# Attention's stages farther apart, one ring for the weights, norms cut into steps: a change to the order of work in a decoder layer on one core

## The chip, the cores and the metric

The kernel runs on one core of a Trainium2 chip. The metric is device time in microseconds (us) of one execution; a kernel's time is the median of several. The core has a matrix engine (TensorE, PE in the rows; PEld is its weight load), three engines for the rest (VectorE or DVE, ScalarE or ACT, GpSimd or POOL), and SyncE (SP), whose only work here is to issue DMAs. Every engine, SP's queue among them, executes its own list of instructions strictly in order, so one that waits holds up all behind it.

## The reference

One layer of a decoder on 2048 tokens of width 1024, all in float32:

```python
mod = silu(c) @ w_ada + b_ada                   # six vectors: shift, scale, gate, twice
shift1, scale1, gate1, shift2, scale2, gate2 = jnp.split(mod, 6, axis=-1)
h = modulate(rms_norm(x, g_mix), shift1, scale1)
proj = h @ w_in                                 # u, v of the gMLP | q (8 heads) | k, v (2 heads)
out_a = chunked_sgu(gelu(z_a), w_spatial, b_spatial)            # chunks of 128 tokens, causal
out_b = sliding_window_sink_attention(q, k, v, sinks, positions) # window 128, rotary
x = x + gate1 * (concat([out_a, out_b]) @ w_out)
h2 = modulate(rms_norm(x, g_ffn), shift2, scale2)
x = x + gate2 * (square(relu(h2 @ w_ff1)) @ w_ff2)              # width 4096
return rms_norm(x, g_final)
```

## The kernel before

The tokens lie in four slabs of 512 (slab 0 to 3), features on the 128 partitions. Every large product is made of three matmuls (`mm3`): an operand is split into a high part (ACT copies it to the matmul's type) and a low part (DVE subtracts), and high times high, high times low and low times high are added up in PSUM. Each slab passes through `in_qkv` (q, k, v, with rotary in `rotate`), `in_vu` (the gMLP), `attention`, `mix_build` and `out_proj` (which also adds up the squares for the next norm). The two feed-forward halves, `ffn_c` (w_ff1) and `ffn_d` (w_ff2), work on a pair of slabs p at once by a scheme of seven products in place of eight; `h2_build` makes their inputs. `ffn_d` goes through products i = 1, 6, 5, 3, 7, 4, 2, each in eight chunks of 24 matmuls; after 7 and after 2 a slab of the output is complete and `final_norm` runs.

The parts are generators that yield between pieces of work, and the program weaves them: `weave(main, side, per=3)` takes three steps of `side` after each step of `main`, `zipped` takes turns, `ratio(a, 3, b, 1)` three of one and one of the other. A scheduler then makes each engine's list from that order. Within `attention` there are eight units (128 tokens and one k/v head each), and each passes four stages: q (split q: tile `qst`), p (scores `sc` on PE, softmax to `pr` on DVE and ACT), t (transposes `tpp` on PE, split to `pc` on ACT and DVE, causal masks to `pp` and `pc` on POOL) and o (`ov` on PE, `os` on ACT and DVE, then a DMA to `mixb`). One loop turns them:

```python
for t in range(n + 3):
    for i in (3, 2, 1, 0):
        if 0 <= t - i < n:
            stages[i](t - i)
            yield
```

so a unit's stage follows three yields after the one before. Tiles come from rings of fixed size, and an allocation waits for the oldest use to end: `wr` (4 tiles of 4 KB a partition) takes raw weights, `wk` (8) their split parts, `xl` (4 of 2 KB) x tiles and the modulation weights `adar`, `m2` (60 of 2 KB) nearly everything else. `ada_rest(ci)` makes one of the modulation vectors 2 to 5: 16 loads, 16 scalings on ACT, 14 additions on POOL (`acc`), 8 small matmuls (`modp`). A norm is `finish` (four small matmuls `msp`, then POOL's power) and `spread` (a diagonal `dg` on DVE, a matmul `bcp`, a copy to `rbc` on ACT). Slab 2's q, k, v are made early, parked in DRAM (`away`) and loaded again (`back`, `qkv_back`); the slabs in the tuple `LATER` do this.

From 907 us on, `ffn_d(0)` is the main line and everything that remains of slabs 2 and 3 (`beside`) is woven into it at three steps a chunk, then `h2_build(1)` at one step a chunk.

Of the kernel before, what the change touches and what calls it, by code (L numbers as in the profile page):

```python
# [49 lines left out]
def hybrid_block(ctx, tc, x_l, c_l, pos, wada0, wada, vec, win, wsT, bs, sinks, wout, w1, w2, rope_c, y_l):  # L50
# [14 lines left out]
    def wk(name, shape=None):  # L65
        return sb.tile(shape or [P, D], F32R, name=name, tag="wk", bufs=NWK)

    def wr(name, shape=None):
        return sb.tile(shape or [P, D], F32, name=name, tag="wr", bufs=NWR)

    def wk4(name, shape):
        return sb.tile(shape, F32R, name=name, tag="wr", bufs=NWR)
# [111 lines left out]
    class Stat:  # L184
# [23 lines left out]
        def spread(self, out=None, tag="ov"):  # L208
            nb = self.n // P
            parts = [small("rh", [P, NB], F32R), small("rl", [P, NB], F32R)]  # L210
            dve.tensor_copy(out=parts[0][:, :nb], in_=self.rs[:, :nb])
# [2 lines left out]
            for i, r in enumerate(parts):
                dg = t2("dg", F32R, [P, NB, P])
                dve.tensor_tensor(out=dg[:, :nb], in0=ident.unsqueeze(1).broadcast_to([P, nb, P]),
                                  in1=r[:, :nb].unsqueeze(2).broadcast_to([P, nb, P]), op=ALU.mult)
                pe.matmul(out=bp[:, :nb], lhsT=ones_r, rhs=dg[:, :nb], start=i == 0, stop=i == 1)
# [1 line left out]
            act.activation(out=rbc[:, :self.n], in_=bp[:, :nb], func=AF.Copy)  # L220
            return rbc[:, :self.n]

        def bcast(self, out=None, tag="ov"):
            self.finish(tag)
            return self.spread(out, tag)
# [566 lines left out]
    def ffn_c(p, forms):  # L792
        raws, wfs = {}, {}

        def split(src, name, home=wk):
            hi, lo = home(name), home(name)
            act.activation(out=hi, in_=src, func=AF.Copy)
            dve.tensor_tensor(out=lo, in0=src, in1=hi, op=ALU.subtract)  # L798
            return hi, lo
# [89 lines left out]
    def ffn_d(p):  # L889
# [26 lines left out]
        for i in (1, 6, 5, 3, 7, 4, 2):  # L916
# [5 lines left out]
            for c in range(8):  # L922
                wraw, araw = wr("w2w"), wr("aw", [P, 2, T])
# [7 lines left out]
                wh, wl, ah, al = wk("w2h"), wk("w2l"), wk("ah", [P, 2, T]), wk("al", [P, 2, T])  # L931
                act.activation(out=wh, in_=wraw, func=AF.Copy)  # L932
                dve.tensor_tensor(out=wl, in0=wraw, in1=wh, op=ALU.subtract)  # L933
                act.activation(out=ah, in_=araw, func=AF.Copy)  # L934
                dve.tensor_tensor(out=al, in0=araw, in1=ah, op=ALU.subtract)  # L935
# [297 lines left out]
```

## Time and profile before

| | |
|---|---|
| median of 3 executions | 2215.06 us (2214.13 to 2216.72) |
| the profiled execution, its own time | 2211.44 us |
| its span, first to last instruction | 2209.7 us (1.7 us lie around it) |
| PE busy | 1965.2 us, 89% of the span |
| DVE, ACT, POOL busy | 1398.8, 936.4 and 244.7 us |
| mean granted TensorE clock | 0.945 |
| DMA | 475.24 MB, mean 215 GB/s |

PE is the engine to follow: it is busy 89% of the time, and the rest of the time it waits for one of the others. Two numbers say what a wait costs: the idle time itself, and the granted clock (PEclk), which is 1.00 (2.4 GHz) in steady work and shows 0.50 (1.2 GHz) in pieces around the waits.

### The profile page before, as it was taken

How to read it: one execution, taken by the hardware profiler on the slowest of the kernel's cores; microseconds unless marked ns; L12 is line 12 of the kernel's file. 1: busy time of each engine (PE TensorE's matmuls, PEld its weight loads, DVE VectorE, ACT ScalarE, POOL GpSimd, SP SyncE). 2: the span in 40 equal slices, each digit the busy share in tenths (PEclk: the TensorE clock that was granted, in tenths of full speed). 3: DMA queues.
4: the chain of work that ended last, by engine and by line, in shares of the span. 5: the costliest groups of instructions: out<-in, count | busy, mean ns of one | idle time of the engine just before them, and what ended most of it. 6: DMA issues, size and time to landing. Idle time of an engine off the chain costs nothing.

```text
span 2209.7 us, 26145 instructions
## 1 busy us (share of the span) xinstructions
PE 1965.2 (89%) x8852; PEld 1604.4 (73%) x8852; DVE 1398.8 (63%) x2342; ACT 936.4 (42%) x1618; POOL 244.7 (11%) x290
## 2 busy tenths in 40 slices
PE   5988788779799999968998998898799999999997
PEld 4777665558677788757786876677688888888775
DVE  7766566624877866666556565279776666444665
ACT  3534444343554444542344243237344444433432
POOL 5223101251030000011001022000000000000000
PEclk9999889789899999989999998999899999999998
DMA  9874474488379945879875764668344445666653
GB/s 365 317 284 149 147 260 152 136 288 289 99 251 308 310 156 167 265 241 317 293 250 177 243 196 160 212 211 282 126 162 157 158 148 175 207 197 216 212 190 133
DMA packets 230391, 475.24 MB, mean 215 GB/s; under 512 B 23617, under 2 KB 81089, under 8 KB 230257
## 3 DMA queue, kind: packets, MB, share of 16 engines
q1 hardware_dynamic: 229136, 472.85, 63.1%
q8 instruction: 70, 1.15, 0.2%
q0 software_dynamic: 1120, 0.72, 0.1%
q14 instruction: 65, 0.52, 0.1%
HBM read 343.78 MB, written 129.70 MB: 214 GB/s over the span
## 4 chain that ended last, share of the span: by engine, by line
PE 49%; DMA 10%; DVE 9%; issue 2%; ACT 2%; POOL 1%; SPq 0%; DVEq 0%; POOLq 0%; ACTq 0%
PE mm L296 16%; PE mm L295 15%; PE mm L297 15%; DMA a<-in_w_dram 3%; DMA w2d<-a 2%; DMA s<-w2d 1%; DVE al L935 1%; DVE hw L726 1%; DMA r<-in_w_dram 1%; DVE w2l L933 1%; DVE y L983 1%; PE ov L646 0%; DVE x L900 0%; DVE ssum L194 0%; ACT pr L606 0%
## 5 line engine op out<-in xcount | busy, mean ns | idle before, releaser
L296 PE MATMUL mm<-al,w2h 128*128 128x512 f32 x896 | 358.9, 401 | 15.7 <-DVE al L935 15.7
L297 PE MATMUL mm<-ah,w2l 128*128 128x512 f32 x896 | 356.4, 398 | 0.0
L295 PE MATMUL mm<-ah,w2h 128*128 128x512 f32 x896 | 313.1, 401 | 12.8 <-DVE pr L591 6.7
L932 ACT ACTIVATE w2h<-w2w 128x1024 fp32r<-128x1024 f32 x112 | 118.6, 1058 | 311.1 <-PE mm L296 270.3
L933 DVE TENSOR_TENSOR w2l<-w2w,w2h 128x1024 fp32r<-128x1024 f32 x112 | 137.8, 1230 | 168.0 <-ACT w2h L932 167.2
L296 PEld LDWEIGHTS mm<-al,w2h 128*128 128x128 f32 x896 | 173.3, 193 | 56.8 <-DVE al L935 21.1
L295 PEld LDWEIGHTS mm<-ah,w2h 128*128 128x128 f32 x896 | 172.0, 193 | 50.9 <-ACT ah L934 7.0
L297 PEld LDWEIGHTS mm<-ah,w2l 128*128 128x128 f32 x896 | 173.0, 193 | 36.2
L295 PE MATMUL mm<-h,whi 128*128 128x512 f32 x320 | 130.8, 425 | 22.5 <-ACT h L233 8.0
L205 POOL TENSOR_TENSOR rs<-ms,mhalf 128x4 f32<-128x4 f32 x12 | 15.8, 1318 | 1195.5 <-DVE ms L203 1195.5
L934 ACT ACTIVATE ah<-aw 128x1024 fp32r<-128x1024 f32 x112 | 117.4, 1048 | 65.5 <-PE mm L296 56.2
L935 DVE TENSOR_TENSOR al<-aw,ah 128x1024 fp32r<-128x1024 f32 x112 | 137.1, 1224 | 7.7 <-ACT ah L934 7.2
L297 PE MATMUL mm<-h,wlo 128*128 128x512 f32 x320 | 131.5, 412 | 5.5 <-POOL wlo L263 3.4
L296 PE MATMUL mm<-h,whi 128*128 128x512 f32 x320 | 132.2, 414 | 0.6 <-DVE h L234 0.6
L295 PE MATMUL mm<-mix,whi 128*128 128x512 f32 x256 | 108.6, 425 | 18.9 <-DVE x L684 13.1
L295 PE MATMUL mm<-hw,wa 128*128 128x512 f32 x256 | 103.2, 403 | 20.5 <-ACT hw L725 12.0
L296 PE MATMUL mm<-mix,whi 128*128 128x512 f32 x256 | 106.1, 415 | 1.8 <-DVE mix L673 1.7
L629 POOL TENSOR_SCALAR_AFFINE_SELECT pp<-pc 128x512 fp32r<-128x512 f32 x60 | 49.1, 818 | 522.0 <-ACT pc L623 509.7
L297 PE MATMUL mm<-mix,wlo 128*128 128x512 f32 x256 | 105.2, 411 | 0.0
L296 PE MATMUL mm<-hw,wa 128*128 128x512 f32 x256 | 102.1, 399 | 1.1 <-DVE hw L726 1.1
L295 PE MATMUL mm<-hw,wb 128*128 128x512 f32 x256 | 100.1, 391 | 2.4 <-DVE w L857 2.3
L297 PE MATMUL mm<-hw,wa 128*128 128x512 f32 x256 | 101.4, 398 | 0.3 <-DVE wa L798 0.3
(255 smaller groups left out, 4451.8 us busy)
## 6 DMA issues: line engine op xcount, KB each, us to landing
aw<-ad SPq DMA_DIRECT2D x112, 512.0 KB, 4.6
r<-in_w_dram SPq DMA_DIRECT2D x64, 512.0 KB, 4.2
w2w<-w2d SPq DMA_DIRECT2D x64, 512.0 KB, 3.6
ad<-wt SPq DMA_DIRECT2D x96, 256.0 KB, 4.3
a<-in_w_dram SPq DMA_DIRECT2D x96, 256.0 KB, 4.7
w2w<-in_w_dram SPq DMA_DIRECT2D x96, 256.0 KB, 3.8
xt<-in_x_dram SPq DMA_DIRECT2D x80, 256.0 KB, 4.2
adar<-in_wada_dram SPq DMA_DIRECT2D x64, 256.0 KB, 4.0
```

Of the source, the lines that this page charges most:

```text
L205: self.pow = pool.tensor_tensor(out=rs[:, :nb], in0=ms[:, :nb], in1=mhalf[:, :nb], op=ALU.pow)
L295: pe.matmul(out=out, lhsT=wh, rhs=h[0], start=first, stop=False, **kw)
L296: pe.matmul(out=out, lhsT=wh, rhs=h[1], start=False, stop=False, **kw)
L297: last_mm[0] = pe.matmul(out=out, lhsT=wl, rhs=h[0], start=False, stop=last, **kw)
L629: pool.affine_select(out=o, in_=i, pattern=[[0, 4], [-1, P]], compare_op=ALU.is_gt, fill=0.0, base=0, channel_multiplier=1)
L726: dve.tensor_tensor(out=lo, in0=f, in1=hi, op=ALU.subtract)
L932: act.activation(out=wh, in_=wraw, func=AF.Copy)
L933: dve.tensor_tensor(out=wl, in0=wraw, in1=wh, op=ALU.subtract)
L934: act.activation(out=ah, in_=araw, func=AF.Copy)
L935: dve.tensor_tensor(out=al, in0=araw, in1=ah, op=ALU.subtract)
L983: dve.scalar_tensor_tensor(out=y, in0=x, scalar=gfin[:, d:d + 1], in1=rbc, op0=ALU.mult, op1=ALU.mult)
```

## The change

It touches five things. (1) The stages of a step of attention run in the order q, p, t, o in place of o, t, p, q, so that a unit's stage follows five yields after the one before. (2) `wr` is gone; raw weights, split weights, the modulation weights (now two tiles a load, 512 KB) and two x tiles of the last norm share one ring `wk` of 12. (3) Norms are cut into `finish`, `diag` and `cast` with yields between; `final_norm` is a generator, stepped between the chunks of `ffn_d` or woven into `ffn_c(1)`. (4) Modulation vector 3 is made beside attention of slab 0, and vector 4 beside `in_qkv(2)`; `out_proj(1)` runs with nothing beside it. (5) Slab 3 joins `LATER`.

```diff
-NT, NM, NWK, NWR, NXL = 9, 60, 8, 4, 4
+NT, NM, NWK, NXL = 9, 60, 12, 4
-LATER = (2,)
+LATER = (2, 3)
...
-                raw = sb.tile([P, T], F32, name="adar", tag="xl", bufs=NXL)
-                nc.sync.dma_start(out=raw, in_=wada[ci - 2, half, k])
+                if k % 2 == 0:
+                    two = wk("adar", F32, [P, 2, T])
+                    nc.sync.dma_start(out=two, in_=wada[ci - 2, half, k:k + 2].rearrange("k p t -> p k t"))
+                raw = two[:, k % 2]
...
-        def spread(self, out=None, tag="ov"):
+        def diag(self):
...
+        def cast(self, out=None, tag="ov"):
...
+        def spread(self):
+            self.diag()
+            return self.cast()
...
-        raw = wr("raw")
+        raw = wk("raw", F32)
...
-            for i in (3, 2, 1, 0):
+            for i in range(4):
                 if 0 <= t - i < n:
                     stages[i](t - i)
                     yield
...
         for s in (2 * p, 2 * p + 1):
-            rb2[s] = rb2[s].spread()
+            rb2[s].diag()
+        yield
+        for s in (2 * p, 2 * p + 1):
+            rb2[s] = rb2[s].cast()
         yield
...
-                raws[j] = wr("r1"), wr("r2")
+                raws[j] = wk("r1", F32), wk("r2", F32)
...
-                xs[r, t, b] = m2("x3", F32)
+                if src is x2d:
+                    xs[r, t, b] = m2("x3", F32)
+                else:
+                    two = wk("x3w", F32, [P, 2, T]) if b % 2 == 0 else two
+                    xs[r, t, b] = two[:, b % 2]
...
-                wraw, araw = wr("w2w"), wr("aw", [P, 2, T])
+                wraw, araw = wk("w2w", F32), wk("aw", F32, [P, 2, T])
...
+                if c > 0:
+                    step(norm)
                 if c < 7:
                     yield
...
             if i == 7:
-                final_norm(2 * p + 1, xs, 1, stats[1])
+                norm = final_norm(2 * p + 1, xs, 1, stats[1])
             if i == 2:
-                final_norm(2 * p, xs, 0, stats[0])
+                last.append(final_norm(2 * p, xs, 0, stats[0]))
             yield
...
     def final_norm(s, xs, t, stat):
-        rbc = stat.bcast(t2("rbc"), tag="sc")
+        stat.finish("sc")
+        yield
+        stat.diag()
+        yield
+        rbc = stat.cast(t2("rbc"), "sc")
+        yield
...
-          chain(then_halo(0, attention(0, st)), mix_build(0, mix), x_stats(2, rn), spread(rn)), per=3)
+          ratio(chain(then_halo(0, attention(0, st)), mix_build(0, mix), x_stats(2, rn), spread(rn)), 5,
+                part(ada, 6), 1), per=3)
...
-    weave(in_qkv(2, hx, sts[2]), chain(att, mix_build(1, mix1), part(ada, 6)), per=3)
-    weave(out_proj(1, mix1), ada)
+    weave(in_qkv(2, hx, sts[2]), chain(att, mix_build(1, mix1), ada), per=3)
+    run(out_proj(1, mix1))
...
         keep_halo(2)
+        yield from qkv_back(3, st3)
...
-    run(ffn_c(1, forms1))
-    run(ffn_d(1))
+    weave(ffn_c(1, forms1), last[0])
+    run(ffn_d(1, last))
+    run(last[1])
```

What that does to the engines' lists is shown at three places. The first is ACT's list in attention of slab 1, which shows the turn of the stages best: `qst` is stage q, `pr` and `es` are stage p, `pc` is the copy of stage t, `os` that of stage o (`h` and `sq` belong to neighbours). Before:

```order
L608 ACTIVATE es<-es 128x4
L623 ACTIVATE pc<-tpp 128x512
L566 ACTIVATE qst<-qr 64x128 x4
L233 ACTIVATE h<-ht,mod 128x512
L649 ACTIVATE os<-ov 64x512
L606 ACTIVATE pr,den<-pr,nm 128x128 x4
L190 ACTIVATE sq<-x_3715 128x512
L608 ACTIVATE es<-es 128x4
L623 ACTIVATE pc<-tpp 128x512
L233 ACTIVATE h<-ht,mod 128x512
L566 ACTIVATE qst<-qr 64x128 x4
L649 ACTIVATE os<-ov 64x512
```

Each `pc` is followed at once by the `os` of the same unit, with only another unit's `qst` between. The change, from the first `pc` of the slab on:

```order
L626 ACTIVATE pc<-tpp 128x512
L236 ACTIVATE h<-ht,mod 128x512
L569 ACTIVATE qst<-qr 64x128 x4
L626 ACTIVATE pc<-tpp 128x512
L323 ACTIVATE vhalo<-vst 128x128
L236 ACTIVATE h<-ht,mod 128x512
L609 ACTIVATE pr,den<-pr,nm 128x128 x4
L611 ACTIVATE es<-es 128x4
L569 ACTIVATE qst<-qr 64x128 x3
L652 ACTIVATE os<-ov 64x512
```

Between the first unit's `pc` and its `os` now stand the next unit's `pc` and a third unit's softmax.

The second place is POOL's list at the start of attention of slab 0 (`acc` are the additions of `ada_rest`, AFFINE_SELECT the masks). Before:

```order
L205 TENSOR_TENSOR rs<-ms,mhalf 128x4
L169 TENSOR_TENSOR acc<-acc,adar 128x512 x14
L633 AFFINE_SELECT pc<-pc 128x512 x4
L395 DMA S_t<-rscr 8x512 x4
L394 DMA C_t<-rscr 8x512 x4
L629 AFFINE_SELECT pp<-pc 128x512 x2
```

And with the change:

```order
L206 TENSOR_TENSOR rs<-ms,mhalf 128x4
L170 TENSOR_TENSOR acc<-acc,adar 128x512 x21
L636 AFFINE_SELECT pc<-pc 128x512 x4
L398 DMA S_t<-rscr 8x512 x4
L397 DMA C_t<-rscr 8x512 x4
L632 AFFINE_SELECT pp<-pc 128x512 x2
L636 AFFINE_SELECT pc<-pc 128x512 x2
L170 TENSOR_TENSOR acc<-acc,adar 128x512 x2
L632 AFFINE_SELECT pp<-pc 128x512 x2
L170 TENSOR_TENSOR acc<-acc,adar 128x512
L636 AFFINE_SELECT pc<-pc 128x512 x2
L170 TENSOR_TENSOR acc<-acc,adar 128x512 x4
```

Seven more additions stand ahead of the first mask and seven among the next ones.

The third place is DVE's list where `ffn_d(0)` ends and `ffn_c(1)` begins (`ms` to `dg` and `y` are the last norm of slab 2, `hw`, `wt`, `hb` are `h2_build(1)`, `s` and `r` prepare the first weights of `ffn_c(1)`). Before:

```order
L203 TENSOR_SCALAR ms<-msp 128x4
L726 TENSOR_TENSOR hw<-wt,hw 128x512
L211 CAST rh<-rs 128x4
L212 TENSOR_TENSOR rl<-rs,rh 128x4
L216 TENSOR_TENSOR dg<-ident,rh 128x512
L216 TENSOR_TENSOR dg<-ident,rl 128x512
L983 SCALAR_TENSOR_TENSOR y<-x_12848,vecs,rbc 128x512
L983 SCALAR_TENSOR_TENSOR y<-x_12850,vecs,rbc 128x512
L983 SCALAR_TENSOR_TENSOR y<-x_12852,vecs,rbc 128x512
L983 SCALAR_TENSOR_TENSOR y<-x_12854,vecs,rbc 128x512
L983 SCALAR_TENSOR_TENSOR y<-xt,vecs,rbc 128x512 x4
L818 TENSOR_TENSOR s_13348<-r_13337 128x512
```

And with the change:

```order
L709 TENSOR_TENSOR hb<-hb 128x512
L710 TENSOR_TENSOR wt<-hb,wt 128x512
L732 TENSOR_TENSOR hw<-wt,hw 128x512 x2
L732 TENSOR_TENSOR hw<-hb,hw 128x512 x2
L732 TENSOR_TENSOR hw<-wt,hw 128x512
L818 TENSOR_TENSOR s_13254<-r_13243 128x512
L819 TENSOR_TENSOR r_13243<-r_13242,r_13243 128x512
L70 TENSOR_TENSOR wcl<-s_13254,wch 128x512
L820 TENSOR_TENSOR r_13242<-s_13254,r_13242 128x512
L821 TENSOR_TENSOR r_13242<-r_13242 128x512
L204 TENSOR_SCALAR ms<-msp 128x4
L818 TENSOR_TENSOR s_13352<-r_13247 128x512
```

The norm moved behind the first weight preparation, and more of `h2_build(1)` moved ahead of it.

## Rows read from the trace of the kernel before

**Rows 1.** The page: span, and busy time of each engine.
```profile
span 2209.7 us, 26145 instructions
PE 1965.2 (89%) x8852; PEld 1604.4 (73%) x8852; DVE 1398.8 (63%) x2342; ACT 936.4 (42%) x1618; POOL 244.7 (11%) x290
```

**Rows 2.** Windows: start and end, length, busy time and count by engine.
```profile
core 0: us, PE busy (x) PEld busy (x) DVE busy (x) ACT busy (x) POOL busy (x), PEclk, DMA share, GB/s
...
150.00:165.00 15.00, 8.74 (x30) 7.35 (x31) 7.05 (x14) 7.48 (x15) 5.82 (x5) 0.66 0.91 341
165.00:290.00 125.00, 96.75 (x508) 80.68 (x508) 74.57 (x212) 58.71 (x156) 33.05 (x42) 0.88 0.43 144
...
345.00:432.00 87.00, 68.57 (x266) 49.74 (x264) 56.41 (x166) 31.94 (x110) 17.37 (x27) 0.86 0.41 137
...
450.00:520.00 70.00, 51.05 (x215) 40.83 (x214) 12.73 (x19) 26.79 (x40) 40.67 (x36) 0.85 0.88 297
...
570.00:596.00 26.00, 12.05 (x42) 8.45 (x41) 25.41 (x44) 15.89 (x28) 0.00 (x0) 0.67 0.30 101
...
955.00:1012.00 57.00, 34.76 (x125) 26.15 (x124) 42.10 (x86) 21.34 (x53) 8.29 (x12) 0.76 0.81 268
...
1190.00:1222.00 32.00, 24.45 (x87) 17.45 (x86) 22.53 (x57) 14.56 (x44) 6.68 (x8) 0.79 0.50 163
...
1310.00:1395.00 85.00, 63.01 (x243) 47.93 (x242) 49.06 (x112) 32.17 (x80) 19.37 (x20) 0.86 0.55 176
...
1454.00:1464.00 10.00, 7.65 (x31) 6.24 (x31) 4.42 (x10) 2.89 (x4) 1.01 (x1) 0.83 0.02 2
...
1552.00:1576.00 24.00, 12.74 (x45) 9.53 (x44) 20.07 (x34) 6.88 (x14) 1.38 (x1) 0.72 0.24 89
1576.00:1870.00 294.00, 294.00 (x1299) 243.32 (x1298) 193.56 (x261) 135.74 (x199) 0.00 (x0) 1.00 0.48 157
...
2095.00:2126.00 31.00, 24.11 (x89) 18.91 (x88) 21.34 (x29) 8.39 (x10) 1.01 (x1) 0.83 0.46 157
```

**Rows 3.** PE's waits: total us, times, longest us.
```profile
PE ov L646 <- POOL pp L629: 29.5, 29, 2.3
...
PE tpp L621 <- DVE pr L612: 17.4, 5, 5.7
PE bcp L218 <- DVE dg L216: 17.3, 7, 3.6
...
PE vp L459 <- ACT va L454: 11.4, 2, 10.4
...
PE modp L174 <- POOL acc L169: 6.3, 1, 6.3
...
PE ov L646 <- POOL pc L633: 5.8, 8, 2.0
PE mm L295 <- ACT mix L672: 5.8, 3, 4.9
```

**Rows 4.** DVE's timeline across the end of ffn_d(0): start, duration, instruction.
```profile
1551.84 0.78 DVE L900 SCALAR_TENSOR_TENSOR x<-mm,mod,x 128x512 f32<-128x512 f32 x1
...
1571.65 0.69 DVE L818 TENSOR_TENSOR s<-r 128x512 f32<-128x512 f32 x1
...
1578.56 1.22 DVE L798 TENSOR_TENSOR wb<-r,wb 128x1024 fp32r<-128x1024 f32 x1
```

**Rows 5.** ada_rest's additions on POOL, and attention's split of q on DVE.
```profile
L169 POOL TENSOR_TENSOR acc<-acc,adar x56: 1259/1289/2156, 141.7 to 635.7; 128x512 f32<-128x512 f32 x56
...
L567 DVE TENSOR_TENSOR qst<-qr,qst x128: 275/285/1352, 166.3 to 1350.9; 64x128 fp32r<-64x128 f32 x128
```

**Rows 6.** DMA from 905 to 1085 us, and the fastest of its 10 us windows.
```profile
DMA packets 29298, 51.13 MB, mean 284 GB/s; under 512 B 2506, under 2 KB 15818, under 8 KB 29287
...
1005.00:1015.00 10.00, 7.60 (x24) 5.81 (x25) 3.88 (x8) 1.21 (x2) 3.21 (x4) 0.66 1.03 395
```

More of the change, by code (lines that the diff above doesn't have):

```diff
@@ L63, in m2, with wk, halve @@
         return sb.tile(shape or [P, T], dt, name=name, tag="m2", bufs=NM)
[L65 to L72, printed above, removed]
+    def wk(name, dt=F32R, shape=None):
+        return sb.tile(shape or [P, D], dt, name=name, tag="wk", bufs=NWK)
+    def halve(t, hi, lo):
+        act.activation(out=hi, in_=t, func=AF.Copy)
+        dve.tensor_tensor(out=lo, in0=t, in1=hi, op=ALU.subtract)
+        return hi, lo
     def small(name, shape, dt=F32):
@@ L206, in finish @@
             self.rs = rs
-        def spread(self, out=None, tag="ov"):
-            nb = self.n // P
+        def diag(self):
             parts = [small("rh", [P, NB], F32R), small("rl", [P, NB], F32R)]
-            dve.tensor_copy(out=parts[0][:, :nb], in_=self.rs[:, :nb])
-            dve.tensor_tensor(out=parts[1][:, :nb], in0=self.rs[:, :nb], in1=parts[0][:, :nb], op=ALU.subtract)
-            bp = ps.tile([P, NB, P], F32, name="bcp", tag=tag, bufs=2 if tag == "sc" else 1)
[L214 to L218, printed above, removed]
-            rbc = m2("rbc", F32) if out is None else out
[L220 to L225, printed above, removed]
+            dve.tensor_copy(out=parts[0], in_=self.rs)
+            dve.tensor_tensor(out=parts[1], in0=self.rs, in1=parts[0], op=ALU.subtract)
+            self.dg = [t2("dg", F32R, [P, NB, P]) for _ in parts]
+            for dg, r in zip(self.dg, parts):
+                dve.tensor_tensor(out=dg, in0=ident.unsqueeze(1).broadcast_to([P, NB, P]),
+                                  in1=r.unsqueeze(2).broadcast_to([P, NB, P]), op=ALU.mult)
+        def cast(self, out=None, tag="ov"):
+            bp = ps.tile([P, NB, P], F32, name="bcp", tag=tag, bufs=2 if tag == "sc" else 1)
+            for i, dg in enumerate(self.dg):
+                pe.matmul(out=bp, lhsT=ones_r, rhs=dg, start=i == 0, stop=i == 1)
+            rbc = m2("rbc", F32) if out is None else out
+            act.activation(out=rbc, in_=bp, func=AF.Copy)
+            return rbc
+        def spread(self):
+            self.diag()
+            return self.cast()
     def h_tile(x, k, rbc, which, inplace=False):
@@ L793, in ffn_c @@
         raws, wfs = {}, {}
[L795 to L799, printed above, removed]
         def load(j):
@@ L813, in prep @@
             if n == 0:
-                x = split(r1, "wa")
+                x = halve(r1, wk("wah"), wk("wal"))
                 wf[1], wf[2] = (x, 0), (x, T)
@@ L887, in hybrid_block, with ffn_d @@
            for r in range(2) for t in range(2) for b in range(4)}
-    def ffn_d(p):
+    def ffn_d(p, last):
+        norm = iter(())
         xs, us, vs = {}, [None] * 4, [None] * 4
@@ L930, in ffn_d @@
                 nc.sync.dma_start(out=araw, in_=ad[p, i, c])
[L931 to L935, printed above, removed]
+                wh, wl = halve(wraw, wk("w2h"), wk("w2l"))
+                ah, al = halve(araw, wk("ah", F32R, [P, 2, T]), wk("al", F32R, [P, 2, T]))
                 for b in range(4):
@@ L985, in final_norm @@
             nc.sync.dma_start(out=y_l[s, d], in_=y)
+            if d % 2:
+                yield
     def run(*gens):
@@ L1032, in x_stats @@
                 yield
+        yield
         stat.finish()
@@ L1037, in spread @@
     def spread(rb):
-        rb.append(rb[0].spread())
+        rb[0].diag()
+        yield
+        rb.append(rb[0].cast())
         yield
@@ L1143, in hybrid_block @@
     h2 = h2_build(0, forms)
+    next(h2)
     next(h2)
@@ L1162, in hybrid_block @@
     side, w2l, h2 = beside(), w2_late(), h2_build(1, forms1)
-    for n, _ in enumerate(ffn_d(0)):
+    last = []
+    for n, _ in enumerate(ffn_d(0, last)):
         if 4 <= n:
```

6 lines of the change are left out of this document (3 added, 3 removed).

## The prediction

> **What bounds the kernel now.** The page's first lines come first: of a span of 2209.7 us PE is busy 1965.2 and DVE 1398.8 [rows 1]. PE decides, so the question is where it stands still. The table of windows answers that. Between 1576 and 1870 us, inside `ffn_c(1)` and the start of `ffn_d(1)`, PE is busy all of 294.00 us at PEclk 1.00 and does 1299 matmuls, 0.226 us each [rows 2]. That is this kernel at full speed; no order of work makes these matmuls cheaper. In any other window two amounts can be won: the idle time (length less PE busy) and what a low clock cost, which I take as (1 - PEclk) times PE busy, since a stretch at 0.50 takes twice as long as at 1.00. I then read which waits fill the idle time, in the list of PE's waits: for each the tile that PE wanted, the engine and tile that came last, total, count and longest [rows 3].
>
> **The change, part by part.**
>
> **(a) Attention's stages.** Five windows hold the pieces of the kernel with most of attention in them: 165–290, 345–432, 955–1012, 1190–1222 and 1310–1395 us [rows 2]. Idle: 28.25 + 18.43 + 22.24 + 7.55 + 21.99 = 98.5 us. Clock: .12 x 96.75 + .14 x 68.57 + .24 x 34.76 + .21 x 24.45 + .14 x 63.01 = 43.5 us. Together 142. The waits which name attention's own chain are `ov` for the masks `pp` and `pc`, 29.5 + 5.8, and `tpp` for the softmax's `pr`, 17.4: 52.7 us, or 53% of the idle time [rows 3]. They have one cause. Before, a unit's stage stands three yields behind the stage that feeds it and with the order o, t, p, q only one other unit's stage is in between; in PE's list 16 of the 32 units have their first `ov` less than 2 us of full-speed PE work behind the last transpose, and that time must hold a copy on ACT, a subtraction on DVE and masks on POOL. With the change 3 units stand so close and the others have 2.6 us or more. From `sc` to `tpp` there were 0.3 to 6 us in the units that wait; now there are 8 or more in all but the last unit, against a longest wait of 5.7 [rows 3]. If all these waits go and take the same share of the clock's cost along, 52.7 + .53 x 43.5 = 76 us. I take two thirds, 50: three units remain close, and behind a wait that goes stands what it covered, DVE with 74.57 us of work in the 125 us of slab 0's window and 42.10 in the 57 of 955–1012 [rows 2], where the same instructions still have to run before PE's next need. Bounds 0 (all of it replaced by other waits) and 142 (neighbouring waits go too).
>
> **(b) `out_proj(1)` without `ada_rest`.** Window 450–520 us: idle 18.95, clock .15 x 51.05 = 7.7, together 26.6 [rows 2]. One wait of 10.4 us, `vp` for `va`, is ACT standing at a scaling whose `adar` tile has not come; the DMA share there is 0.88 [rows 2, 3]. The change takes the vector's loads away from here, and puts them beside `in_qkv(2)`, where they hold up to 8 of 12 ring tiles while that part's weights are loaded as well. I take 20 of 26.6; bounds 0 and 26.6.
>
> **(c) The eight `modp` matmuls.** Before, PE waits 6.3 us once for POOL's additions [rows 3]; window 150–165: idle 6.26 and .34 x 8.74 = 3.0, together 9.3 [rows 2]. With `ada_rest` as a sixth of the turns beside attention of slab 0 these matmuls stand about 11 us of PE work later. I take 8; bounds 0 and 9.3.
>
> **(d) Norms in steps.** The end of product 7 of `ffn_d(1)`, 2095–2126: 6.89 + .17 x 24.11 = 11.0. The burst of folds stays, the norm's `dg` and `bcp` move behind the next chunk: 5. The seam from `ffn_d(0)` to `ffn_c(1)`, 1552–1576: 11.26 + .28 x 12.74 = 14.8 [rows 2]. DVE's chain from the first fold at 1551.84 to the end of the first `wb` at 1579.78 is 28 us; in it the eight `y` and the norm's small steps stand ahead of the weights' `s` at 1571.65 [rows 4]. In the new list the `y` are gone from there, but 20 of `h2_build(1)`'s additions (as `s`, 0.69 us a piece [rows 4]) still stand between the folds and `s`; the chain becomes some 9 us shorter and PE still outruns it. I take 6. Window 1454–1464, the norm after product 7 of `ffn_d(0)`: 2.35 + 1.3 = 3.7; I take 3. Sum 14; bounds 0 and 29.5.
>
> **(e) What it costs.** Ahead of the first weights of `ffn_c(0)`, seven more additions of `w2_early`, 0.69 each [rows 4], now stand on DVE, which is busy 25.41 of 26.00 us in 570–596 [rows 2]: no cover, 5. Fourteen additions of `ada_rest` move into attention of slab 0, 1.29 us each on POOL [rows 5]. They can cost nothing (POOL is busy 33.05 of 125 us) or hold up DVE each time, 14 x 1.29 = 18. That two engines get in each other's way shows in this trace: DVE's split of q takes 285 ns as a rule and up to 1352, POOL's addition 1289 and up to 2156 [rows 5]. DVE has 40% of that window free; I take 3.
>
> The Trainium skill, SBUF — State Buffer, section "Who interferes with whom", speaks against this move: a DVE instruction with two inputs in SBUF and a GpSimd one that reads SBUF exclude each other for the whole instruction. By that rule the cost would lie nearer 18 than nothing, and the net gain nearer 62 than 77. The trace agrees that there is such a conflict, 1352 ns against 285 [rows 5], but not that every pair meets.
>
> Since `ada_rest` fills one turn in six, attention, `mix_build(0)` and the sums for slab 2's norm end later; what remains runs after the main line with nothing beside it. The nearest row is `mm` for `mix`, 4.9 us at longest [rows 3]: 4. Slab 3's q, k and v go through DRAM and come back: 12 transfers of 256 KB, 3.1 MB; at 284 GB/s [rows 6] 11 us of DMA, while other work runs. Their loads stand in SP's queue, ahead of the later weights; with two of twelve ring tiles held by `x3w` through product 2, I take 3. Where the new waits of the one ring cost nothing, it is because PE is a chunk of 24 matmuls (5.4 us) behind the splits; what it costs if that cover goes is rival C. Sum of (e) 15; bounds 0 and 45 (5 + 18 + 11 + 11).
>
> **Sum.** 50 + 20 + 8 + 14 - 15 = 77 us. The profiled execution's own time, 2211.4 us, is 3.6 below the median of 2215.1; 2211.4 - 77 = 2134, and on the median's scale 2138 us.
>
> **The rivals.**
>
> **A, a fuller recovery.** Waits for ACT in attention (`qst`, `os`, gelu) have the same close spacing as cause; with them 110 of attention's 142 us come back and the net is 137: 2078 us. For it: the named waits are only 53% of the idle time, and the clock falls for every one. Against: in the five windows DVE is busy 58 to 74% of the time [rows 2], and cannot follow much faster.
>
> **B, the bottleneck beside `ffn_d(0)` is elsewhere.** From 905 to 1085 us 51.13 MB pass, at 284 GB/s on the mean and 395 in the fastest 10 us, with DMA shares of 0.81 and 1.03 [rows 2, 6]. Slab 3's trip adds to it, and a PE that waits less reaches the DMA sooner. Then the gains in the last three windows are lost, half of (a), 25 (they hold 74 of its 142), and half of (d), 7, and 5 come on top as waits for loads: 77 - 37 = 40, 2175 us. Against: at 395 GB/s 51.13 MB take 129 of the 180 us.
>
> The Trainium skill, DMA: Bandwidth & Descriptors, section "Where 436 GB/s comes from", gives about 358 GB/s a core for transfers with HBM; by it 51.13 MB take an estimated 143 us. The window with 395 GB/s [rows 6] is above that figure; either way transfers alone do not fill these 180 us.
>
> **C, slower: one ring starves the chunks of `ffn_d(0)`.** A chunk takes six ring tiles (two raw, four split), two chunks that overlap need 10 to 12. Before, raw and split had 4 and 8 of their own. Now `adar`, side weights `raw` and `x3w` take from the same twelve, and a raw tile held by a side step that waits holds up the next allocation in the order of the list. Were four gone, the next chunk's splits could start only when the chunk before ends: two splits of 1.22 us each (as `wb` [rows 4]) before PE may go on, 2.4 us a chunk, and for 56 chunks 134 us: 2215 - 77 + 134 = 2272. It decides from 77 / 56 = 1.4 us a chunk. Against: the sides' weights are only there part of the time, and SP's loads run ahead.
>
> **D, the waits only move.** Since stages also stand ahead of DVE and ACT work that others need, new waits as large as the old arise, and the gains of (b) to (d) are the size of (e): 2211 to 2219. For it is only that DVE's total work does not change.
>
> **How the numbers follow.** Likeliest 0.48, and its own range is 2110 to 2165: (a) between 25 and 76 with the others as taken. A 0.20, B 0.20, C 0.09, D 0.03. The range that should hold 8 in 10 leaves out the upper end of C and half of A's lower tail: 2065 to 2200. A change under 0.2%, 4.4 us, can't be told from none here. Faster 0.88, same 0.03 (D), slower 0.09 (C).
>
> **What the profile after would show.** (a) right: the `ov` waits for `pp` and `pc` and `tpp` for `pr` leave the head of PE's list of waits, and attention's stretches show PEclk of 0.95 and more. Wrong: the same idle time there with DVE, or a DMA, named instead. (b) right: `out_proj(1)`'s 192 matmuls take some 44 us (192 x 0.226) without a wait for `va`; wrong: waits for weights in `in_qkv(2)`. (c): no `modp` wait of 6 us. (d): no `bcp` wait for `dg` after product 7, and at the seam PE still waits some 9 us for `wb`. (e): a longer wait at `ffn_c(0)`'s first product, `acc` beside slow `qst` in slab 0. C would show as short waits for `al` or `ah` once in each chunk of `ffn_d(0)`, with ACT's or SP's queue standing for a tile. The prediction falls most easily by (a): if the waits that remain have another cause, its two thirds are the wrong share, in either direction.

## The result and the profile after

| | before | after |
|---|---|---|
| median | 2214.6 us (4 runs) | 2125.5 us (2121.3 to 2129.1, 4 runs) |
| ratio | | 0.960 (95% interval 0.957 to 0.963) |
| span of the profiled execution | 2209.7 us [rows 1] | 2120.2 us |

The forecast was 2138 (2065 to 2200), likeliest case 2110 to 2165. The sum came out within 13 us; its terms did not, as the experiments show, so the match is in part luck. The page of the changed kernel, its first lines (columns as in [rows 1]):

```profile
span 2120.2 us, 25995 instructions
...
PE 1930.0 (91%) x8852; PEld 1586.7 (75%) x8852; DVE 1423.8 (67%) x2342; ACT 949.4 (45%) x1621; POOL 242.5 (11%) x290
```

PE's list holds the same number of instructions, 8852 matmuls and as many weight loads; its busy time falls by 35 us, and the mean granted clock is 0.959 in place of 0.945. To say where the time came from, both programs are cut at the same matmuls, the first of each part of the main line, so that a stretch holds the same work in both. Before (windows; columns as in [rows 2]):

```profile
0.00:128.80 128.80, 97.72 (x513) 83.27 (x514) 91.53 (x148) 50.48 (x82) 47.81 (x80) 0.97 0.93 342
128.80:445.30 316.50, 251.92 (x1148) 199.72 (x1147) 203.92 (x518) 137.01 (x356) 70.04 (x85) 0.88 0.53 181
445.30:518.20 72.90, 53.97 (x221) 42.95 (x219) 13.77 (x22) 27.78 (x43) 40.00 (x36) 0.86 0.87 292
518.20:907.00 388.80, 366.27 (x1704) 302.08 (x1705) 280.62 (x400) 186.48 (x284) 23.21 (x17) 0.98 0.65 220
907.00:1499.20 592.20, 524.07 (x2362) 426.30 (x2361) 356.52 (x692) 228.01 (x456) 60.26 (x70) 0.93 0.70 234
1499.20:1547.70 48.50, 42.58 (x174) 32.83 (x172) 48.50 (x67) 35.19 (x51) 0.00 (x0) 0.96 0.80 277
1547.70:1871.70 324.00, 312.07 (x1362) 256.93 (x1363) 218.99 (x300) 144.93 (x215) 1.38 (x1) 0.98 0.46 152
2092.00:2149.10 57.10, 50.20 (x204) 40.50 (x203) 35.90 (x46) 19.71 (x22) 1.01 (x1) 0.91 0.56 184
```

They are: start and slab 0's products; the products of slabs 1 and 2 around `out_proj(0)`, with attention of slabs 0 and 1 beside them; `out_proj(1)`; `in_vu(2)` and `ffn_c(0)`; the first six products of `ffn_d(0)`; its last; `ffn_c(1)`; product 4 of `ffn_d(1)`, ahead of which product 7 ends. After, the same stretches:

```profile
0.00:148.30 148.30, 107.27 (x525) 89.35 (x526) 91.79 (x153) 60.26 (x98) 46.73 (x80) 0.91 0.88 304
148.30:420.20 271.90, 227.60 (x1152) 188.34 (x1152) 215.75 (x510) 149.71 (x373) 89.64 (x101) 0.93 0.64 217
420.20:472.50 52.30, 48.90 (x214) 39.12 (x213) 23.56 (x29) 8.64 (x14) 20.10 (x20) 0.97 1.00 366
472.50:862.70 390.20, 365.73 (x1698) 302.91 (x1697) 280.10 (x396) 187.81 (x281) 23.01 (x16) 0.97 0.63 216
862.70:1418.90 556.20, 509.20 (x2362) 416.87 (x2360) 368.64 (x706) 232.69 (x463) 59.73 (x70) 0.96 0.76 259
1418.90:1478.80 59.90, 51.53 (x192) 39.57 (x193) 44.14 (x58) 30.65 (x42) 0.00 (x0) 0.89 0.61 206
1478.80:1789.30 310.50, 306.58 (x1344) 253.46 (x1344) 212.77 (x297) 149.32 (x218) 1.32 (x1) 0.99 0.46 155
2009.60:2058.50 48.90, 46.11 (x203) 36.99 (x202) 35.60 (x45) 20.61 (x22) 1.01 (x1) 1.00 0.68 217
```

Since a stretch holds the same matmuls (but for a few that cross a border, see the counts), its length is the measure. The lengths with those of the experiments' kernels, in us; the sums are the spans:

| stretch | before | turn_only | turn_old | wide_old | after | ada_old | two_rings | norms_old | best_b |
|---|---|---|---|---|---|---|---|---|---|
| start, slab 0 | 128.8 | 129.5 | 149.2 | 146.4 | 148.3 | 146.9 | 128.9 | 149.6 | 136.4 |
| slabs 1, 2; attention 0, 1 | 316.5 | 259.2 | 323.7 | 278.0 | 271.9 | 254.3 | 272.2 | 272.5 | 254.8 |
| `out_proj(1)` | 72.9 | 75.8 | 47.0 | 51.5 | 52.3 | 58.1 | 65.8 | 50.9 | 59.0 |
| `in_vu(2)`, `ffn_c(0)` | 388.8 | 389.4 | 392.6 | 390.3 | 390.2 | 390.8 | 387.6 | 387.3 | 394.5 |
| `ffn_d(0)`, six products | 592.2 | 552.7 | 597.1 | 563.5 | 556.2 | 567.3 | 569.4 | 559.3 | 552.5 |
| its last, and `ffn_c(1)` | 372.5 | 374.1 | 367.6 | 368.4 | 370.4 | 368.5 | 357.8 | 363.4 | 363.2 |
| `ffn_d(1)` | 338.0 | 337.6 | 331.5 | 330.8 | 330.9 | 330.7 | 328.2 | 341.9 | 331.2 |
| sum | 2209.7 | 2118.3 | 2208.7 | 2128.9 | 2120.2 | 2116.6 | 2109.9 | 2124.9 | 2091.6 |

From before to after 89.5 us go. Most went in the two stretches with attention (44.6 and 36.0) and in `out_proj(1)` (20.6); the start became 19.5 longer.

PE's waits after (total us, times, longest us), against [rows 3]:

```profile
PE msp L201 <- DVE ssum L195: 19.5, 3, 11.9
PE mm L298 <- ACT ah L69: 17.4, 11, 2.5
PE mm L299 <- DVE al L70: 13.8, 16, 2.3
PE tpp L624 <- DVE pr L615: 13.1, 9, 6.1
PE mm L298 <- ACT mix L675: 12.9, 4, 7.9
PE bcp L221 <- DVE dg L215: 12.4, 5, 4.8
...
PE sc L591 <- DVE qst L570: 7.6, 4, 5.5
...
PE ov L649 <- POOL pp L632: 1.4, 3, 0.8
...
PE vp L462 <- ACT va L457: 0.2, 1, 0.2
```

The waits of `ov` for the masks are all but gone (29.5 and 5.8 before, 1.4 and 0.5 now), and so is `vp` for `va`. The one of `tpp` for `pr` is not: 13.1, against 17.4. But it is another wait: before, 16.0 of it lay in the six products of `ffn_d(0)`, where 0.4 is left, and 1.4 in the stretch with attention 0 and 1, where 12.7 stand now. At the top stands `msp`, for the sums of squares `ssum`, 19.5 us as before. Behind it come `ah` and `al`, the split of a chunk's operand in `ffn_d`: 31.2 us now and 20.3 before, of which 19.6 and 9.3 lie in the six products of `ffn_d(0)`. Beside `ffn_d(0)` the DMA rate rose: in the first 178 us (862 to 1040) it is 305 GB/s, against 284 in the 180 us of [rows 6], and no wait for a load leads the list.

```profile
DMA packets 30540, 54.23 MB, mean 305 GB/s; under 512 B 2643, under 2 KB 15975, under 8 KB 30528
```

### The profile page after: what moved, and what is told of

Its sections match the earlier page's. It is cut to its first block, busy times and chain, and to the rows that moved or that the text cites. A ratio compares the mean times of both kernels' runs of the same rounds, so it can differ in the third digit from the quotient of the medians.

```text
span 2120.2 us, 25995 instructions
## 1 busy us (share of the span) xinstructions
PE 1930.0 (91%) x8852; PEld 1586.7 (75%) x8852; DVE 1423.8 (67%) x2342; ACT 949.4 (45%) x1621; POOL 242.5 (11%) x290
## 5 line engine op out<-in xcount | busy, mean ns | idle before, releaser
L298 PE MATMUL mm<-ah,w2h 128*128 128x512 f32 x896 | 316.9, 400 | 19.4 <-ACT ah L69 17.4
L206 POOL TENSOR_TENSOR rs<-ms,mhalf 128x4 f32<-128x4 f32 x12 | 13.5, 1123 | 1200.3 <-DVE ms L204 908.8
L298 PE MATMUL mm<-h,whi 128*128 128x512 f32 x320 | 128.2, 416 | 20.6 <-ACT h L236 7.8
L299 PE MATMUL mm<-h,whi 128*128 128x512 f32 x320 | 130.4, 409 | 7.4 <-DVE h L237 7.4
L298 PE MATMUL mm<-hw,wah 128*128 128x512 f32 x256 | 102.8, 403 | 19.0 <-ACT hw L731 10.3
L298 PE MATMUL mm<-mix,whi 128*128 128x512 f32 x256 | 104.9, 412 | 16.0 <-ACT mix L675 12.9
L299 PE MATMUL mm<-mix,whi 128*128 128x512 f32 x256 | 104.0, 407 | 3.5 <-DVE mix L676 3.5
L299 PE MATMUL mm<-hw,wah 128*128 128x512 f32 x256 | 102.5, 400 | 2.6 <-DVE hw L732 2.6
L300 PE MATMUL mm<-hw,wal 128*128 128x512 f32 x256 | 101.9, 399 | 0.8 <-DVE wal L70 0.8
L298 PE MATMUL mm<-hw,wbh 128*128 128x512 f32 x256 | 99.8, 390 | 0.9 <-DVE w L857 0.9
L299 PE MATMUL mm<-hw,wbh 128*128 128x512 f32 x256 | 99.8, 390 | 0.0
```

Of the source, the lines that this page charges most:

```text
L206: self.pow = pool.tensor_tensor(out=rs[:, :nb], in0=ms[:, :nb], in1=mhalf[:, :nb], op=ALU.pow)
L298: pe.matmul(out=out, lhsT=wh, rhs=h[0], start=first, stop=False, **kw)
L299: pe.matmul(out=out, lhsT=wh, rhs=h[1], start=False, stop=False, **kw)
L300: last_mm[0] = pe.matmul(out=out, lhsT=wl, rhs=h[0], start=False, stop=last, **kw)
```

## The experiments

Medians and ratios to the kernel before, which ran beside each group (2213 to 2215 us):

| kernel | median | ratio (95%) |
|---|---|---|
| after | 2125.5 | 0.960 (0.957 to 0.963) |
| turn_only | 2120.2 | 0.959 (0.957 to 0.960) |
| turn_old | 2210.3 | 0.999 (0.998 to 1.000) |
| wide_old | 2129.3 | 0.961 (0.959 to 0.964) |
| ada_old | 2116.2 | 0.956 (0.954 to 0.958) |
| two_rings | 2109.8 | 0.953 (0.951 to 0.955) |
| first_loads | 2117.4 | 0.956 (0.953 to 0.958) |
| x3_late | 2115.5 | 0.957 (0.955 to 0.958) |
| later2 | 2109.5 | 0.953 (0.952 to 0.954) |
| norms_old | 2129.1 | 0.963 (0.959 to 0.966) |
| turn_x3w | 2118.4 | 0.957 (0.954 to 0.960) |
| best_a | 2118.2 | 0.956 (0.954 to 0.958) |
| best_b | 2089.8 | 0.944 (0.941 to 0.947) |

**The turn taken back, and alone.** turn_old is the changed kernel with this edit; turn_only is the kernel before with its reverse.

```diff
-            for i in range(4):
+            for i in (3, 2, 1, 0):
```

> The changed kernel with one line put back: attention's stages run in the order o, t, p, q again. Theory: this turn is what freed PE in attention, so the time rises by 50 to 75 us over the 2125 of the changed kernel, to 2175 to 2200, and the waits of ov for the masks pp and pc return at about 30 us in all. Rival: the single ring, the moved modulation vectors and slab 3's way through DRAM gave attention its gain, so the time stays within 15 us of 2125.

> The kernel before with the order of the stages alone changed to q, p, t, o. Theory: the turn works by itself, 2215 falls to 2140 to 2165. Rival: it needs the other parts (loads and DVE work stand in its way), and the time stays above 2200.

Both moved the way of the theory, and by more: the turn alone takes 93 us off the kernel before (2120.2 against 2213.2), and without it the other four parts together bring 3 us, which the interval doesn't tell from nothing. Nor do they bring anything on top of the turn: the changed kernel, which has all five, is at 2125.5 and the turn alone at 2120.2. In turn_only the waits of attention's own chain are:

```profile
PE ov L646 <- POOL pp L629: 4.5, 7, 1.6
...
PE tpp L621 <- DVE pr L612: 1.0, 1, 1.0
PE ov L646 <- POOL pc L633: 0.8, 2, 0.5
```

These are 6.3 us, so 46 of the 52.7 us of [rows 3] are gone. The two stretches with attention are 57.3 and 39.5 us shorter, 96.8 in all. Of these 54.8 are idle time (64.6 to 35.8 and 68.1 to 42.1, length less PE busy) and 42.0 is PE's busy time, which falls for the same matmuls as the granted clock rises from 0.88 to 0.95 and from 0.93 to 0.96:

```profile
129.50:388.70 259.20, 223.39 (x1148) 184.37 (x1147) 204.66 (x516) 132.32 (x351) 69.11 (x85) 0.95 0.62 217
853.90:1406.60 552.70, 510.56 (x2361) 417.19 (x2360) 361.26 (x692) 227.35 (x456) 64.13 (x70) 0.96 0.75 251
```

**Distance or turn?** wide_old keeps the old turn and puts a unit's stages two rounds apart:

```diff
-        for t in range(n + 3):
-            for i in range(4):
-                if 0 <= t - i < n:
-                    stages[i](t - i)
+        for t in range(n + 6):
+            for i in (3, 2, 1, 0):
+                if 0 <= t - 2 * i < n:
+                    stages[i](t - 2 * i)
```

> The changed kernel with the old turn o, t, p, q, but the stages of a unit two rounds apart in place of one, so that each follows seven yields after the one before (three with the old turn, five with the new). Theory: what counts is the distance between a stage and the one that feeds it; the waits of ov for the masks and of tpp for pr are as short as with the new turn, and the time is 2115 to 2140. Rival: what counts is the turn within a round, that the next unit's scores stand on PE ahead of the transposes and of ov; then the time stays above 2180.

2129 us, 81 less than turn_old with the same turn. So it is the distance, and either way of getting it will do; seven yields bring no more than five.

```profile
PE ov L649 <- POOL pp L632: 5.1, 7, 1.4
...
PE tpp L624 <- DVE pr L615: 2.7, 4, 1.3
...
PE ov L649 <- POOL pc L636: 2.4, 2, 1.3
```

**The modulation vectors.** ada_old undoes part 4 of the change, two_rings undoes part 2 (raw weights in four tiles of their own, split ones in eight, `adar` one 256 KB block a load among the x tiles; `x3w` stays with the split weights and is fetched behind chunk 6).

```diff
-          ratio(chain(then_halo(0, attention(0, st)), ..., spread(rn)), 5, part(ada, 6), 1), per=3)
+          chain(then_halo(0, attention(0, st)), ..., spread(rn)), per=3)
...
-    weave(in_qkv(2, hx, sts[2]), chain(att, mix_build(1, mix1), ada), per=3)
-    run(out_proj(1, mix1))
+    weave(in_qkv(2, hx, sts[2]), chain(att, mix_build(1, mix1), part(ada, 6)), per=3)
+    weave(out_proj(1, mix1), ada)
```

> The changed kernel with the modulation vectors where they stood before: none beside attention of slab 0, vector 3 beside in_qkv of slab 2, vector 4 beside out_proj of slab 1. Theory: out_proj of slab 1 gets its 20 us back as loss, and attention and out_proj of slab 0 lose 10 less: 2130 to 2140. Rival: the wait there came from the small tiles of adar, which are two to a load now, and the time stays at 2115 to 2125.

The rival was right: 2116. `out_proj(1)` with the vector beside it again takes 58.1 us, not 73, and there is no wait for `va`. two_rings, with nothing beside `out_proj(1)` but small `adar` tiles in the stretch ahead, has that wait and takes 65.8:

```profile
PE vp L463 <- ACT va L458: 8.5, 1, 8.5
```

So the gain there comes mostly from the larger loads in the larger ring together (72.9 to 58.1; which of the two is not shown), and the move adds the rest (58.1 to 52.3). The move has a price in the stretch with attention 0 and 1: 271.9 with it, 254.3 without. All that moved stands in these 17.6 us: fourteen additions, their loads, ACT's scalings (ACT is busy 149.71 us against 132.59) and fifteen more matmuls. DVE is busy 215.75 us there in the changed kernel and 205.62 in ada_old, with 510 and 509 instructions, the wait of `tpp` for `pr` is 12.7 against 6.2, and the same 52 splits of q take longer. The changed kernel, then ada_old (groups by line, from slab 1's first product to slab 2's):

```profile
L570 DVE TENSOR_TENSOR qst<-qr,qst 64x128 fp32r<-64x128 f32 x52 | 21.5, 458 | 0.7
```

```profile
L570 DVE TENSOR_TENSOR qst<-qr,qst 64x128 fp32r<-64x128 f32 x52 | 15.0, 337 | 0.6
```

Of the kernels without the move ada_old has the shortest splits; the others have means of 372 (before) to 418 ns (best_b), those with it 458 to 502.

**The one ring.** For two_rings:

> The changed kernel with rings as before: raw weights in four tiles of their own, split weights in eight, adar one row block a load among the x tiles; x3w stays in the ring of split weights, and is taken behind chunk 6. Theory: the one ring costs time at the start (20 us of loss in slab 0's products) and in the last product of the first ffn_d (8 us), and gives nothing back: 2095 to 2108, slab 1's first product at about 130 us. Rival: the one ring gains elsewhere in the first ffn_d by letting loads run farther ahead, and the time is 2115 or more though the start is early.

The start is the theory's: slab 1's first product begins at 128.9 us, as before. The cause stands in SP's list. Before, the first four raw weights are loaded in one go. The one ring hands out raw, high, low, raw, high, low in turn, so a raw weight's load stands behind the parking in DRAM of the high part of the one before (`ki8h`), which waits for that one's split. SP's list (start, duration, instruction) in the kernel before, and in the changed one:

```profile
11.25 2.35 SPq L254 DMA_DIRECT2D raw<-in_win_dram  x4
```

```profile
11.15 0.33 SPq L257 DMA_DIRECT2D raw<-in_win_dram  x1
...
19.00 0.33 SPq L278 DMA_DIRECT2D ki8h<-whi  x1
19.62 0.33 SPq L257 DMA_DIRECT2D raw<-in_win_dram  x1
20.34 0.38 SPq L278 DMA_DIRECT2D ki8l<-wlo  x1
26.82 0.33 SPq L278 DMA_DIRECT2D ki9h<-whi  x1
27.20 0.42 SPq L257 DMA_DIRECT2D raw<-in_win_dram  x1
```

SP's waits in the first 150 us of the kernel before, and of the changed one:

```profile
SPq L275 <- ACT whi L262: 8.2, 4, 4.3
```

```profile
SPq L278 <- ACT whi L265: 39.0, 11, 6.4
```

The gain in all is 16 us, 2 us short of what was expected, since the smaller rings lose 13.5 in `out_proj(1)`, where the one ring does give back. The six products of `ffn_d(0)` are 13 longer too, but so are they by 11 in ada_old, where their code is that of the changed kernel. first_loads takes and loads the first four raw tiles ahead of their splits:

```diff
-        for g in gs_:
-            w0[g] = w_split(first[g], g >= 4, pool if g in (3, 5) else dve)
+        raws = [w_raw(first[g]) for g in gs_]
+        for g, raw in zip(gs_, raws):
+            w0[g] = w_split(first[g], g >= 4, pool if g in (3, 5) else dve, raw)
```

> The changed kernel, with the raw tiles of the first four weights taken and loaded before any of their split tiles is taken from the ring. Theory: the changed kernel loses some 20 us in slab 0's products because one ring hands out raw, high, low, raw, high, low in turn, so the next raw weight is loaded only behind the split of the one before; with the loads first the time falls by 12 to 20 us, to 2105 to 2113, and the first product of slab 1 starts at about 130 us in place of 148. Rival: the late start is DMA rate, another wait or chance, and the time stays within 5 us of 2125.

Missed: slab 1's first product begins at 140.8, 7.5 us of the 19.5, and the median falls by 8, with an interval that overlaps that of the changed kernel. The loads of weights 5 to 7 still stand behind the parking of the first three, and those of the next seven (`ki0`, `ki1`, `ki3` to `ki7`) one by one behind the parking of each other: the last of these is issued at 87.3 us before, at 106.8 here and at 114.3 in the changed kernel. The order of loads is part of the cause; that it is all of it is not shown by this run.

**The ring tiles of `x3w`.**

```diff
-            elif i == 2 and p == 0:
-                fetch(x3d, 0, 0)
...
+                if c == 6 and i == 2 and p == 0:
+                    fetch(x3d, 0, 0)
```

> The changed kernel, with the two ring tiles x3w taken behind chunk 6 of the last product of the first ffn_d, not ahead of its first chunk. Theory: with ten of twelve tiles left a chunk's loads come too late, PE waits 1 to 2 us for al in most chunks; the loss in that product falls from 16 to about 8 us and the time to 2115 to 2120. Rival: the work of h2_build on DVE is what makes al late, and the waits and the time stay.

2115.5, as the theory has it: the last product takes 51.8 us in place of 59.9, with the same matmuls, at PEclk 1.00 in place of 0.89. PE's waits for `al` and `ah` in it are 5.2 us in 7 times, against 10.7 in 8.

```profile
1420.10:1471.90 51.80, 46.51 (x193) 35.34 (x193) 45.09 (x59) 30.23 (x42) 0.00 (x0) 1.00 0.77 256
```

**Slab 3 not through DRAM** (`LATER = (2,)`, no `qkv_back(3)`).

> The changed kernel without slab 3's way through DRAM. Theory: the trip only shifts waits: the 14 us that product 3 of the first ffn_d loses more than before (a wait of 5.5 us for qst and one of 3.0 for pr) go, and some 10 come back in products 6 and 5, so the time is within 10 us of 2125. Rival one: the trip is a plain cost, 2105 to 2112. Rival two: it frees tiles that slab 3's products need, and without it the time is 2140 or more.

The time is rival one's, 16 us less by the medians. Product 3 of `ffn_d(0)`, in the changed kernel and in later2, where the waits of `sc` for `qst` (5.5) and for `pr` (3.9) are missing:

```profile
1134.20:1248.60 114.40, 104.26 (x473) 86.82 (x472) 72.04 (x156) 46.14 (x106) 12.01 (x15) 0.93 0.62 219
```

```profile
1139.00:1237.70 98.70, 95.62 (x445) 79.66 (x444) 62.38 (x132) 38.18 (x87) 12.84 (x14) 0.98 0.67 235
```

That is 15.7 us, but with 28 matmuls fewer, and these come earlier now: products 1, 6 and 5 hold 28 more and are 8.7 us longer (280.2 against 271.5). All six products together are only 5.8 us shorter, and the spans differ by 11.6. So the theory's shift is in the trace as well, and how much of the 16 us is a plain cost of the trip is not shown.

**The norms in one piece.** norms_old runs `final_norm` through where it stood, `spread` in one step in `h2_build`, and `ffn_c(1)` alone.

> The changed kernel with the norms in one piece again, at their old places. Theory: product 7's end in the second ffn_d gets back 8 us of loss and the seam to the second ffn_c 9 us, and the last chunks of the first ffn_d lose up to 3 less: 2136 to 2142. Rival: the seam's gain comes from the earlier first weights or from the ring, and the time is within 6 us of 2125.

The time is the rival's, 2129. Product 4 of `ffn_d(1)` takes 61.1 us in place of 48.9, more than the 8 expected; but the last product of `ffn_d(0)` with `ffn_c(1)` takes 363.4 in place of 370.4, so with the norm in one piece the seam keeps its gain. In all 4 us, which the intervals don't tell from nothing. So something else freed the seam. turn_x3w tries one candidate: turn_only with the four x tiles of the last norm of `ffn_d(0)` taken from the ring (behind chunk 6), not from `m2`.

> The kernel before with two things changed: the turn of the stages, and the four x tiles of the last norm of the first ffn_d taken from the ring of split weights (behind chunk 6), not from m2. Norms stay in one piece. Theory: at the seam to the second ffn_c it was not the norm in one piece that held up the first weights, but m2: their tile s could only follow the y that read the x tiles; with x3w elsewhere s stands ahead of y on DVE, the loss of the second ffn_c falls from 16.8 to 6 to 8 us, and the time from 2120 with the turn alone to 2108 to 2113. Rival: the norm in one piece still keeps PE at msp and bcp there, as in the kernel before, the loss stays at 14 or more, and the time at 2118 to 2122.

Between the two: the last product and `ffn_c(1)` take 369.7 us (49.5 and 320.2) in place of 374.1, and the time, 2118.4, is not clear of 2120.2. On DVE `s` now stands ahead of the norm, which is still in one piece; from the first fold to `wb` it takes 11 us, against the 28 of [rows 4]:

```profile
1464.16 0.74 DVE L904 SCALAR_TENSOR_TENSOR x3w<-mm,mod,x3w 128x512 f32<-128x512 f32 x1
...
1466.09 0.68 DVE L818 TENSOR_TENSOR s<-r 128x512 f32<-128x512 f32 x1
...
1474.02 1.22 DVE L798 TENSOR_TENSOR wb<-r,wb 128x1024 fp32r<-128x1024 f32 x1
```

In the changed kernel the same chain takes 19 us, from 1475.65 to 1494.96, with eleven instructions of `h2_build(1)` ahead of `s`:

```profile
1475.65 0.75 DVE L905 SCALAR_TENSOR_TENSOR x3w<-mm,mod,x3w 128x512 f32<-128x512 f32 x1 [1.77 <-PE mm L300]
...
1488.57 0.69 DVE L818 TENSOR_TENSOR s<-r 128x512 f32<-128x512 f32 x1
...
1493.74 1.22 DVE L70 TENSOR_TENSOR wbl<-r,wbh 128x1024 fp32r<-128x1024 f32 x1
```

**Two versions put together.**

> A version put together from what seemed to pay: the new turn of the stages, norms in steps, both remaining modulation vectors beside in_qkv of slab 2 and none beside attention of slab 0 or out_proj of slab 1; rings as before with x3w behind chunk 6, slab 3 not through DRAM. Theory, from the losses by part of the kernels so far: 2120 with the turn alone, less 20 for out_proj of slab 1, less 18 for the norms at two seams, 2080 to 2092. Rival: twelve steps of modulation beside in_qkv of slab 2 keep ACT from its work there, 2100 to 2115.

Missed, 2118: with small `adar` tiles twelve steps beside `in_qkv(2)` are too many, the last loads and additions run on into `out_proj(1)`, which takes 93.3 us, with `modp` waiting up to 12.9 us for POOL.

> A version put together from the losses by part: the changed kernel with the seven first raw weights in half tiles among the x tiles (all loaded ahead of the first parked split), x3w taken behind chunk 6, slab 3 not through DRAM, modulation vectors where they stood before but through the one ring. Theory: less 19 us in slab 0's products, 8 in the last product of the first ffn_d, 11 for slab 3's trip and 3 to 13 for the vectors: 2074 to 2090. Rival: the parts shift the waits in the first ffn_d against each other, so that only the start is gained, 2095 to 2108.

2089.8 (2085.7 to 2094.8), the fastest of all: 5.6% below the kernel before, 36 us below the changed one. Slab 1's first product begins at 136.4 us. It is changed from after by three of the edits above (x3_late, later2, ada_old) and this one:

```diff
+    def w_raw(key):
+        raw = [m2("raw0", F32) for _ in range(2)]
+        for i, t in enumerate(raw):
+            nc.sync.dma_start(out=t, in_=win[key[1]][:, i * T:(i + 1) * T])
+        return raw
...
-    w_first(0, 1, 2, 3)
+    raw0 = [w_raw(first[g]) for g in range(4)]
     ada.append(ada_first_load(1))
+    raw0 += [w_raw(first[g]) for g in range(4, 7)]
+    w_first(0, 1, 2, 3)
```

## Why the prediction was right, and where it was not

The total was right because a gain taken too small met costs taken too small: (a) was 47 us short, and all else, taken as +27, came to -7. That the two errors nearly cancelled was luck. Term by term, by the lengths in the table:

| step | taken | measured | by |
|---|---|---|---|
| (a) the turn | 50 | 97 | before to turn_only, two stretches |
| (b) `out_proj(1)` | 20 | 21 | before to after |
| (c) `modp`, with (e)'s additions and start of `out_proj(0)` | 8 - 3 - 4 | -13 | turn_only to after, stretch of attention 0 and 1 |
| (d) norms | 14 | 2 + 7 | before to after, the last two lines |
| (e) `ffn_c(0)` | -5 | -1 | before to after |
| (e) slab 3's trip, rest of `ffn_d(0)` | -3 | -4 | turn_only to after, six products |
| the start | 0 | -20 | before to after |

Unrounded these add up to the 89.5 of the spans. Two terms don't fall on one line: of the 14 of (d), 3 were for the norm after product 7 of `ffn_d(0)` and lie in the six products, and the -3 of the last (e) took in the ring tiles of `x3w`, whose 7 us lie in (d)'s line.

**(a)** had the right mechanism, distance (wide_old), and the wrong size. The discount to two thirds was the error, and the clock's share: 46 of 52.7 us of the named waits went, 8 us of other idle time with them, and the low clock, for which I had counted 23 with these waits, gave back 42. The five windows were also too narrow for that sum: by the prediction's rule the two stretches lose 67 us to the clock, not 43.5. From turn_old to after the two stretches give 93, so the size holds with the other parts in place. Rival A, neighbours too, had 110: it was nearer than the likeliest case. The caution about DVE did not hold: its work fits into the shorter stretch (203.92 us in 316.5 before, 204.66 in 259.2 with the turn). Of the signs that were named for the profile, the `ov` waits went, but `tpp` for `pr` stands at 13.1 us, and PEclk is 0.93 and 0.96 in the two stretches. turn_only has 1.0 of that wait and ada_old 6.2, so other parts of the change brought it, the moved vector about half.

**(b)** had the right size, and half the reason. I put the gain down to taking the loads away; 15 of the 21 come with the twelve-tile ring and two blocks a load (ada_old).

**(c)** The wait of 6.3 us left the list, but what was won was paid for in the same stretch by what moved there. I took 3 for their conflict with DVE out of bounds 0 to 18; ada_old without them is 17.6 shorter there. How much of that is the conflict, and how much the loads, scalings and matmuls that moved with the additions, no run separates.

The Trainium skill, SBUF — State Buffer, section "Who interferes with whom", has a DVE instruction with two SBUF inputs and a reading GpSimd instruction exclude each other. The trace agrees in kind: 10 us more DVE time for nearly the same instructions, qst 458 ns against 337 to 418. By that rule the bound of 18 was the nearer end, and the stretch came out there, though not by the conflict alone as far as is shown.

**(d)** 9 for 14, and not by the steps I named. Norms in steps give 12 behind product 7 against norms_old, and 8 against the kernel before, where 5 was taken. At the seam they are not what frees the first weights: moving the x tiles out of `m2` gives 4 (turn_x3w) of some 9 (372.5 before, 363.1 in x3_late), and holding two of twelve ring tiles through the last product takes 7 back. That is rival C on a small scale, `al` or `ah` late in most chunks of one product (10.7 us in 8 waits; before 5.9 in 6). In the other six it came about in part at most: 16 such waits in 48 chunks, 19.6 us against 9.3 before and 11.8 in turn_only. Rival B did not come about: transfers ran faster, 305 GB/s, and PE gained.

**The start** is the step that is missing altogether. I asked what the one ring does where raw and split tiles compete for room, in `ffn_d(0)`, and not what its order of handing out does to the order of loads where room is plenty.

**Slab 3's trip** is the least settled: 4 by one comparison, 16 by the medians of later2 and after, of whose profiled executions the six products show 6.

Open: why first_loads and best_b recover only 7.5 and 12 of the start's 19.5; the other half of the seam; and why the first six products of `ffn_d(0)` take between 556 and 567 us in kernels whose code there is the same (after 556.2, x3_late 558.2, first_loads 559.9, ada_old 567.3). To the first the traces give a hint: in best_b the first seven raw weights are all issued by 25.2 us, ahead of any parking, but the next seven still go one by one, the last at 103.1 us, against 87.3 before and 85.2 in two_rings. No run moves these loads alone. And a part's effect of some 10 us in those six products can't be read from one kernel.

## What to carry to other kernels

Where engines run their lists in order, count for each hand-over how much of the waiting engine's work lies between, and stretch the short ones first: here one line of loop order was worth all of the change (93 of 89 us). A ring shared by tiles that are loaded and tiles that are computed also sets the order of the loads, so take the loaded tiles first. When several edits come together, price each alone and measure each alone; a total that fits says little on its terms.

## What was not expected of the hardware

Short waits cost nearly as much again through the clock: turn_only removes 55 us of idle time, none of the waits for masks longer than 2.3 us and none of `tpp` for `pr` longer than 5.7 [rows 3], and the same matmuls then take 42 us less, at granted clocks of 0.95 and 0.96 in place of 0.88 and 0.93. I had counted on 23. POOL's additions did not clearly pay for the move as DVE did: their median is 1375 ns against 1289 before [rows 5], but 1353 in ada_old, without the move, and 1294 in two_rings, with it.
